# Four buffers for the routing steps' entries and slots, and the last tiles' routing step moved into the tile loop

## The chip, the cores and the metric

The kernel runs on one core of a Trainium2 chip. The metric is device microseconds (us) of one execution, the median of several. The engines are PE (matmul; its weight loads are shown as PEld), DVE (vector), ACT (scalar), POOL (GpSimd) and SP (here it only issues DMAs). Each works through its own queue in order.

## What is computed

One layer of a decoder over 2048 tokens of 1024 features: four token mixers, an output projection with a norm, then a mixture of experts with a gated embedding beside it, and a second norm. The change touches the routing of the experts, which in the reference is

```python
group_p, group_idx = lax.top_k(group_prob, 1)              # best of 4 groups
e_logits = (xt @ w_re + b_re).reshape(t_tok, 4, 8)
e_logits = take_along_axis(e_logits, group_idx[:, :, None], axis=1)[:, 0]
expert_p, local_idx = lax.top_k(softmax(e_logits), 2)      # best two of its 8 experts
gate = group_p * expert_p / sum(expert_p)
expert_idx = group_idx * 8 + local_idx
# ... tokens sorted by expert; each expert's rows: (silu(x Wg) * (x Wu)) Wd, times gate, added up by token
x = LN(alpha * x + HMoE(x) + sigmoid(x W_g + b_g) * (p[i] @ W_p))
```

## The kernel before

The tokens are 16 tiles of 128. After the mixers, `out_proj` (line 1384) makes the first norm's output of all tiles, `ple` (line 1557) makes router logits, gates and embeddings tile by tile and writes each token into the lists of its two experts, and `moe` (line 1851) goes through 32 experts in turns of some 30 us: gate and up weights and down weights are loaded and split into two parts, rows are gathered by the list, multiplied, and added to the rows of `accd` in memory. `finish` is the second norm.

In `ple`, `LATE` is 4, so E = 12 and L = 9. Tiles 0 to 8 go through the loop `for t in range(L)`: `turn` transposes a tile on PE and splits it (ACT, DVE line 52), `gates` multiplies it by the 1060 columns of router and gate in three groups (24 matmuls a group and tile, line 1588; group 0 holds the 36 logits, which line 1592 puts into `r_lg`), `embed` multiplies `p` by its weights and writes the tile to `accd` (lines 1595 to 1611). Tiles 12 to 15 give only their logits, in the turns 1, 3, 5 and 7 of the loop. Tiles 9, 10 and 11 come after the loop: first group 0 of each, then groups 1 and 2 with the embedding of each.

Routing goes by four tiles. `route` (line 1470) is some 40 small DVE instructions and two on ACT: it picks group and experts and fills `r_ent` (token number and gate of 4 tiles x 2 experts) and a one-hot matrix `r_oh`. `route_place` (line 1515) is two matmuls with `r_oh`, some 17 DVE instructions that count slots up to `r_idx`, and 8 indirect DMAs of POOL (line 1541), which scatter the entries `r_ent` to the slots `r_idx` of the lists `listd`. The order of the placings is tiles 0-3, 4-7, 12-15, 8-11. When all are written, `lists` (line 1692) reads the lists' heads back by one DMA of SP (line 1698) into a buffer of the pool `wide`, transposes them on PE (line 1707) and makes the index tables; line 1776 gathers the first expert's rows into another `wide` buffer. That pool has three buffers, which the gates of tiles 9, 10 and 11 hold until their writes to `accd` have landed.

The routing's tiles come from the pool `pw` (line 1562), with one buffer each. So a `route` that writes `r_ent` waits until the 8 scatters of the placing before it have read it.

The order on each engine is not the program's: a planner sets it before the run, by place in the program and by the times of a model, and may take an instruction early where its inputs are ready. Between runtime branches of the experts' stage it moves nothing across.

Of the kernel before, what the change touches and what calls it, by code (L numbers as in the profile page):

```python
# [30 lines left out]
class Layer:  # L31
# [44 lines left out]
    # feature-major column tiles of w_in (start column, width)  # L76
# [4 lines left out]
    # columns that the token shift mixes, with their place in its weights  # L81
# [20 lines left out]
    def proj(self, h, blocks):  # L102
        """one half of the tokens against some of the columns, a block at a time"""
# [91 lines left out]
    # the columns that a causal convolution and silu follow  # L195
    CONV = "mq0", "mq1", "mk0", "mk1"

    def conv(self, i, p, y, more):
        """the taps carry a factor 1/2"""
        nc = self.nc  # L200
        nc.scalar.activation(y, p, AF.Identity, scale=self.cw[:, i, 3:4], bias=self.cb[:, i:i + 1])
        for t in range(3):
            s, w = 3 - t, self.cw[:, i, t:t + 1]
            nc.vector.scalar_tensor_tensor(y[:, s:512], p[:, 0:512 - s], w, y[:, s:512], op0=OP.mult, op1=OP.add)
            if more:
                nc.vector.scalar_tensor_tensor(y[:, 0:s], self.last[:, i, t:3], w, y[:, 0:s], op0=OP.mult, op1=OP.add)
        nc.vector.tensor_copy(self.last[:, i], p[:, 509:512])
        nc.scalar.activation(p, y, AF.Tanh)
        nc.vector.scalar_tensor_tensor(y, p, 1.0, y, op0=OP.add, op1=OP.mult)  # L209

# [62 lines left out]
    def sigmoid(self, out, in_, bias=0.0):  # L273
        """out = 0.5 + 0.5 tanh((in + bias2)/2), bias = bias2 / 2"""
        self.nc.scalar.activation(out, in_, AF.Tanh, bias=bias, scale=0.5)
        self.nc.gpsimd.tensor_scalar(out, out, 0.5, 0.5, op0=OP.mult, op1=OP.add)
# [34 lines left out]
    def rwkv_consts(self):  # L311
# [28 lines left out]
        # masks over [j, i]: same chunk of 64, strict / inclusive, block off the 32-diagonal  # L340
# [19 lines left out]
        # row mu of partition quarter s holds row m = 4 mu + s of the transposed inverse  # L360
# [7 lines left out]
        # products of a tile's tokens, zero between its two chunks  # L368
# [11 lines left out]
    def rwkv_pre(self, q):  # L380
        """scaled operands of the chunks and the inverses of the diagonal 32-blocks"""
# [112 lines left out]
    def rwkv_a(self, q, tt):  # L494
        """token-major operands and the masked products of a tile's chunks, four heads together"""
# [30 lines left out]
    def rwkv_b(self, q, tt):  # L526
        """solves, the chain over the chunks, the tile's outputs"""
# [92 lines left out]
    def rwkv(self):  # L620
        """the group in steps: operands run ahead of the products, and these ahead of the chain"""
# [45 lines left out]
    def log_sigmoid(self, z, out, t):  # L667
        """out = min(z, 0) - ln(1 + exp(-|z|)) for z in SBUF"""
# [22 lines left out]
    def gla_pre(self, q):  # L691
        """queries and keys times their chunk's decays, which go out to memory"""
# [86 lines left out]
    def gla_general(self):  # L779
        """Token by token, for decays too strong for the chunks' common scale."""  # L780
# [67 lines left out]
    def mlstm_gates(self):  # L848
        """gates of all chunks of 128, rows 16 h + c, and the running maxima"""
        nc = self.nc  # L850
        with ExitStack() as ctx:
# [39 lines left out]
            # own chunk's decay on the channels of each head  # L891
# [117 lines left out]
    def rope_tables(self):  # L1009
        """cos and sin (negated for the first half of a head's pairs) of position * frequency, for four heads' rows"""  # L1010
# [36 lines left out]
    def mla_consts(self):  # L1047
# [4 lines left out]
        # the heads' first 64 columns; their rotary columns; these with the pairs swapped  # L1052
# [10 lines left out]
        # the heads' key columns, then their value columns  # L1063
# [16 lines left out]
        # adds the two halves of the rows  # L1080
# [13 lines left out]
    def mla_norms(self, q):  # L1094
        """one over the latents' norms"""
# [22 lines left out]
    def mla_latents(self, q, cn, rs):  # L1118
        """latents over their norms; from them the values of all heads, and their queries and keys, which go out to memory"""
# [62 lines left out]
    def mla_query(self, hd, q):  # L1182
        """queries in two parts with the negated row maxima below them, in steps"""
# [11 lines left out]
        # any value near a row's maximum serves its softmax alike: the leading parts give it  # L1195
# [29 lines left out]
    def mla_attend(self, hd, q):  # L1225
        """even key tiles' products in the upper half of the rows, odd ones' in the lower half, at the same time"""
# [48 lines left out]
    def mla(self):  # L1275
        """the attention of a block of queries in steps, the next block's queries and keys made beside it"""
# [24 lines left out]
        for i, (hd, q) in enumerate(blocks):  # L1301
            while at <= i:
                at = next(ahead, 99)
            for _ in self.mla_attend(hd, q):
                work += self.LEAD
                # a head's keys lie over those of the head before the last
# [12 lines left out]
    ALPHA = 2.0 ** 0.25  # L1319

    def late_pools(self, ctx):
        """first norm's outputs in pairs of tiles, over them later an expert's gate and up weights; transposed blocks"""
# [9 lines left out]
    def weights(self, parts, n, scale=None, pool=None):  # L1332
        """128 rows of weights, put side by side, in leading and trailing parts"""
# [8 lines left out]
    def transpose_split(self, src, hi, lo, spread=False):  # L1342
        """[128, n] to [128, n/128, 128] in leading and trailing parts, rows 0 .. 63 and 64 .. 127 by turns in case of spread"""
# [113 lines left out]
    def pick(self, vals, mx, io, n, k, name):  # L1457
        """lowest index among the entries equal to the maximum, and its one-hot"""
# [11 lines left out]
    def route(self, t0, n, lg):  # L1470
        """tokens of tiles t0 .. t0 + n from logits [128, n, 36]"""
# [28 lines left out]
        ent = w.tile([128, 2, n, 2], F32, name="r_ent")  # L1500
# [14 lines left out]
    def route_place(self, r):  # L1515
        """slots in the experts' lists, behind those of the earlier tiles"""
# [20 lines left out]
        ix = w.tile([128, 2, n], I32, name="r_idx")  # L1537
# [9 lines left out]
    # columns of router and gate side by side, in groups that fill a bank  # L1547
# [9 lines left out]
    def ple(self):  # L1557
        nc, I = self.nc, self.I
        with ExitStack() as ctx:
# [13 lines left out]
            def turn(t):  # L1573
                X[t] = self.turned(self.x1[t]) if t < L + 2 else self.turned(self.x1[t], c)
# [38 lines left out]
            def expert(k, i):  # L1613
                """half of a piece of the first expert's gate and up weights, over rows that are done with"""
# [7 lines left out]
            def logits(t):  # L1622
                """of a tile whose gate comes last; its rows of the experts' sums start from the residual"""
# [14 lines left out]
            for t in range(L):  # L1638
# [11 lines left out]
                if t % 4 == 3:  # L1650
                    r = self.route(t - 3, 4, LG.pop(t // 4))
                if t in (4, 5):
                    expert(0, t % 4)
# [5 lines left out]
            r = self.route(E, 4, LG.pop(E // 4))  # L1659
            gates(L, (0,))  # L1660
            turn(L + 2)
            gates(L + 1, (0,))
            gates(L + 2, (0,))
            self.route_place(r)
# [15 lines left out]
    # of the second norm's tiles: which have their sums taken by ScalarE, and which are scaled by VectorE alone  # L1680
# [4 lines left out]
    NB = 3  # L1685

    def slots(self, ids, gates, idx, gate):
        """a list's entries: token numbers, halved gates"""
# [3 lines left out]
    def lists(self, lt):  # L1692
        """rows of the lists' first blocks: token numbers and gates, one slot per partition"""
# [7 lines left out]
        for j, (i, k) in enumerate(((0, 0), (0, 1), (1, 1), (2, 0))):  # L1701
            if i and k:
                # rows of a full block after one spreading of its columns and after two
# [14 lines left out]
        def pick(j, i):  # L1718
            """part j of the entries for a first block or one of up to 64 rows, part i for others"""
# [11 lines left out]
        # counts in the experts' order of turns, and the higher one of each expert's and the last one's before it  # L1731
# [14 lines left out]
    # experts take turns by group, since the tokens crowd into some of the groups  # L1746
    ORDER = [i % 4 * 8 + i // 4 for i in range(32)]

    def raw_gu(self, e, k):
        """two 128-row pieces of the gate and up weights of the expert that comes in turn e, side by side"""  # L1750
# [28 lines left out]
    def moe_banks(self):  # L1779
        """banks that keep a value when a block is passed over"""  # L1780
# [6 lines left out]
    def passes(self, x, wh, wl, k, half):  # L1787
        """products of the parts; of 64 rows, both parts stand side by side and their products 64 rows apart"""
# [5 lines left out]
    def moe_gu(self, x, W, banks, piece=None, half=False):  # L1794
        """x times gate and up weights, all pieces or one"""
# [8 lines left out]
    def fold(self, p, m):  # L1804
        """adds the lower half's products to the upper half's where m is 1"""
# [6 lines left out]
    def moe_h(self, banks, gate, t=None):  # L1812
        """silu(g) * u * gate, the factor 1/2 of the silu in the gate"""
# [31 lines left out]
    def moe_put(self, y, idx):  # L1845
        """adds rows to those of their tokens; an empty slot's token is out of bounds"""
# [4 lines left out]
    def moe(self, G0=(), x0=None, experts=32):  # L1851
# [8 lines left out]
        def load_counts(t, e, engines):  # L1860
            """four experts' counts, loaded behind the last expert's instructions"""
# [46 lines left out]
        def sized(e, b, f):  # L1908
            """f(False) for more than 64 rows in a block, f(True) for up to 64"""
# [16 lines left out]
        def third(e):  # L1926
            """the third blocks: an expert's products with its down weights and the next one's with gate and up weights"""
# [74 lines left out]
    def moe_general(self):  # L2002
        """the lists' further blocks, for experts with more tokens than the static blocks hold"""
# [48 lines left out]
    def late_x(self, t):  # L2052
        """the first norm's outputs of two tiles whose gates come last"""
# [229 lines left out]
```

## Time and profile before

| | us |
|---|---|
| median of three runs | 3141.1 |
| lowest and highest | 3138.97, 3142.75 |
| span of the profiled execution | 3146.7 |
| PE busy in it, share of the span | 2840.9, 90% |
| logits and gates of tiles 0 to 8, up to | about 1970 |
| tiles 9 to 11 and the lists, from there up to the first expert's first matmul | 2050.87 |

The profiled execution has its span as its only time; it is 5.6 us (0.2%) above the median. In the profile a row of the timeline gives start, length, engine, line of the kernel, operation, what is written and read, and in brackets the engine's idle time just before and what ended it.

### The profile page before, as it was taken

How to read it: one execution, taken by the hardware profiler on the slowest of the kernel's cores; microseconds unless marked ns; L12 is line 12 of the kernel's file. 1: busy time of each engine (PE TensorE's matmuls, PEld its weight loads, DVE VectorE, ACT ScalarE, POOL GpSimd, SP SyncE). 2: the span in 40 equal slices, each digit the busy share in tenths (PEclk: the TensorE clock that was granted, in tenths of full speed). 3: DMA queues.
4: the chain of work that ended last, by engine and by line, in shares of the span. 5: the costliest groups of instructions: out<-in, count | busy, mean ns of one | idle time of the engine just before them, and what ended most of it. 6: DMA issues, size and time to landing. Idle time of an engine off the chain costs nothing. (4 is left out here: it accounts for less than half of the span.)

```text
span 3146.7 us, 42893 instructions
## 1 busy us (share of the span) xinstructions
PE 2840.9 (90%) x15420; PEld 2248.3 (71%) x15421; DVE 1955.0 (62%) x4094; ACT 1225.4 (39%) x2001; POOL 896.7 (28%) x552
## 2 busy tenths in 40 slices
PE   8999999998999899999999998789889988998883
PEld 6888888777877665566577797677667766776662
DVE  6366543566555466766656643467576767666869
ACT  4223232222134332323310121166575756666753
POOL 1000100111010033324421200346355545554525
PEclk9999999999998898989999998899999999999996
DMA  6332143122133612200243412188587867777873
GB/s 189 104 87 75 48 129 92 51 56 59 49 93 132 189 33 69 58 27 17 88 143 132 141 60 60 41 295 275 181 269 233 294 216 237 267 251 225 287 243 134
DMA packets 287054, 443.17 MB, mean 141 GB/s; under 512 B 84088, under 2 KB 152040, under 8 KB 286760
## 3 DMA queue, kind: packets, MB, share of 16 engines
q1 hardware_dynamic: 272200, 397.78, 38.3%
q0 software_dynamic: 14560, 41.47, 5.4%
q8 instruction: 184, 3.01, 0.4%
q14 instruction: 110, 0.90, 0.1%
HBM read 350.52 MB, written 96.50 MB: 142 GB/s over the span
## 5 line engine op out<-in xcount | busy, mean ns | idle before, releaser
L1801 PE MATMUL m_g<-m_g,xhl 128*128 128x512 f32 x2032 | 516.6, 402 | 14.7 <-PEq L1928 8.0
L1801 PEld LDWEIGHTS m_g<-m_g,xhl 128*128 128x128 f32 x2032 | 373.6, 191 | 105.9 <-issue 29.8
L1772 DVE TENSOR_TENSOR m_g<-m_raw,m_g 128x1024 fp32r<-128x1024 f32 x188 | 263.7, 1429 | 124.3 <-ACT m_g L1771 78.9
L1771 ACT CAST m_g<-m_raw 128x1024 fp32r<-128x1024 f32 x252 | 255.3, 1057 | 120.8 <-PEq L1928 105.3
L1833 PE MATMUL m_y<-m_dh,m_h 128*128 128x512 f32 x672 | 236.0, 415 | 24.6 <-PEq L1928 6.1
L59 PE MATMUL pbank<-xh,wh 128*128 128x512 f32 x544 | 220.7, 406 | 11.5 <-DVE us L209 8.2
L60 PE MATMUL pbank<-xl,wh 128*128 128x512 f32 x544 | 219.3, 403 | 0.0
L61 PE MATMUL pbank<-xh,wl 128*128 128x512 f32 x544 | 218.3, 402 | 0.0
L51 ACT CAST xhl<-bank 128x512 fp32r<-128x512 f32 x204 | 118.2, 607 | 251.6 <-PE bank L1350 244.0
L1772 POOL TENSOR_TENSOR m_g<-m_raw,m_g 128x1024 fp32r<-128x1024 f32 x64 | 182.8, 2940 | 89.6 <-ACT m_g L1771 50.5
L1408 PE MATMUL wide<-wt,xhl 128*128 128x512 f32 x768 | 183.4, 397 | 3.6 <-ACT xhl L51 3.6
L1772 POOL TENSOR_TENSOR m_dl<-m_raw,m_dh 128x1024 fp32r<-128x1024 f32 x64 | 177.9, 2814 | 22.1 <-ACT m_dh L1771 21.9
L1833 PEld LDWEIGHTS m_y<-m_dh,m_h 128*128 128x128 f32 x672 | 134.9, 201 | 58.7 <-issue 9.0
L1408 PEld LDWEIGHTS wide<-wt,xhl 128*128 128x128 f32 x768 | 143.7, 189 | 40.1 <-ACT xhl L51 7.4
L1248 POOL TENSOR_TENSOR mla_acc<-mla_acc,mla_pt 128x512 f32<-128x512 f32 (+3 forms) x112 | 135.7, 1212 | 117.4 <-ACT mla_pt L1246 101.1
L52 DVE TENSOR_TENSOR xhl<-bank,xhl 128x512 fp32r<-128x512 f32 x204 | 136.4, 685 | 49.3 <-ACT xhl L51 47.0
L1847 POOL DMA_INDIRECT accd<-m_y,m_put x47 | 94.6, 2013 | 249.6 <-ACT m_y L1840 135.5
L1588 PE MATMUL gate<-wt,xhl 128*128 128x354 f32 (+1 forms) x864 | 152.1, 333 | 14.3 <-DVE wide L1593 7.8
L1246 ACT ACTIVATE mla_pt<-sbank 128x512 f32<-128x512 f32 (+3 forms) x160 | 85.1, 533 | 202.7 <-PE sbank L1242 118.0
L1588 PEld LDWEIGHTS gate<-wt,xhl 128*128 128x128 f32 x864 | 144.1, 193 | 16.5 <-DVE wide L1593 8.6
L1833 PE MATMUL m_y<-m_dl,m_h 128*128 128x512 f32 x376 | 153.9, 409 | 0.0
L59 PE MATMUL pbank<-wh,xh 128*128 128x256 f32 x512 | 151.2, 295 | 0.0
(635 smaller groups left out, 6340.8 us busy)
## 6 DMA issues: line engine op xcount, KB each, us to landing
m_raw<-in_moe_w_down SPq DMA_DIRECT2D x64, 1024.0 KB
m_raw<-in_moe_w_gate SPq DMA_DIRECT2D x126, 512.0 KB
m_raw<-in_moe_w_up SPq DMA_DIRECT2D x126, 512.0 KB
wraw<-in_w_in SPq DMA_DIRECT2D x80, 256.0 KB
o_x<-in_x SPq DMA_DIRECT2D x16, 512.0 KB
x1d<-m_g SPq DMA_DIRECT2D x16, 512.0 KB
accd<-wide SPq DMA_DIRECT2D x16, 512.0 KB
m_raw<-accd SPq DMA_DIRECT2D x7, 1024.0 KB
```

The costliest lines, as they stand in the source:

```text
L51: nc.scalar.copy(hi, src)
L52: (eng and nc.gpsimd or nc.vector).tensor_sub(lo, src, hi.bitcast(F32))
L59: nc.tensor.matmul(out, lh, rh, start=start, stop=False)
L60: nc.tensor.matmul(out, lh, rl, start=False, stop=False)
L61: nc.tensor.matmul(out, ll, rh, start=False, stop=stop)
L1248: (nc.vector if kt in self.SUMS else nc.gpsimd).tensor_add(acc[:, c0 * 128:512], acc[:, c0 * 128:512], pt[:, 0:n])
L1408: nc.tensor.matmul(p[:, j], a[:, k], W[k][bb][:, j * 512:j * 512 + 512], start=k == 0 and i == 0, stop=k == 7 and i == 2)
L1588: nc.tensor.matmul(p[:, 0:n], a[:, k], b[:, o:o + n], start=k == 0 and i == 0, stop=k == 7 and i == 2)
L1771: self.nc.scalar.copy(h[:, i], raw[:, i])
L1772: lo_eng.tensor_sub(l[:, i], raw[:, i], h[:, i].bitcast(F32))
L1801: self.mark["pe"] = self.nc.tensor.matmul(banks[:, j], a, b[:, k % 2, j * 512:j * 512 + 512], start=k == 0 and i == 0, stop=k == 7 and i = ...
L1833: self.nc.tensor.matmul(p[:, j], a, b[:, k % 2, j * 512:j * 512 + 512], start=k == 0 and i == 0, stop=k == 3 and i == len(ps) - 1)
```

## The change

`r_ent` and `r_idx` get four buffers each. The routing of tiles 12 to 15 moves from behind the loop to the end of turn 8 in it, ahead of the first expert's second piece of weights, and its placing moves from behind the logits of tile 11 to ahead of those of tile 10. The calls of `gates`, `embed`, `lists` and the other two routings stay. (The diff also drops comments.)

```diff
-        ent = w.tile([128, 2, n, 2], F32, name="r_ent")
+        ent = w.tile([128, 2, n, 2], F32, name="r_ent", bufs=4)
...
-        ix = w.tile([128, 2, n], I32, name="r_idx")
+        ix = w.tile([128, 2, n], I32, name="r_idx", bufs=4)
...
                 if t % 4 == 3:
                     r = self.route(t - 3, 4, LG.pop(t // 4))
+                if t == L - 1:
+                    r = self.route(E, 4, LG.pop(E // 4))
                 if t in (4, 5):
                     expert(0, t % 4)
                 if t == L - 1:
...
             turn(L)
             turn(L + 1)
-            r = self.route(E, 4, LG.pop(E // 4))
             gates(L, (0,))
             turn(L + 2)
+            self.route_place(r)
             gates(L + 1, (0,))
             gates(L + 2, (0,))
-            self.route_place(r)
             r = self.route(E - 4, 4, LG.pop(E // 4 - 1))
```

## Rows read from the trace of the kernel before

**Rows 1.** The page's first line: the profiled span.

```profile
span 3146.7 us, 42893 instructions
```

**Rows 2.** Waits, 1965 to 2052: waiter <- awaited: total us, times, longest.

```profile
DVE r_ent L1502 <- DMA listd<-r_ent,r_idx: 20.2, 2, 11.2
...
PE gate L1588 <- DVE wide L1593: 7.8, 1, 7.8
...
PE gate L1588 <- DVE xhl L52: 5.8, 1, 5.8
```

**Rows 3.** Windows: stretch, length, busy PE, PEld, DVE, ACT, POOL, clock, DMA.

```profile
1985.00:1990.00 5.00, 0.00 (x0) 0.00 (x0) 0.51 (x5) 0.00 (x0) 0.11 (x1) 0.66 0.01 0
1996.00:2003.00 7.00, 7.00 (x46) 7.00 (x45) 6.80 (x47) 0.42 (x2) 1.92 (x2) 1.00 0.00 0
2015.40:2023.20 7.80, 0.00 (x0) 0.00 (x0) 5.77 (x25) 0.07 (x1) 0.90 (x1) 0.62 0.06 22
```

**Rows 4.** Timeline of DVE: one-hots and entries of 12-15 and 8-11, the lists' first copy.

```profile
1978.17 0.28 DVE L1512 TENSOR_TENSOR r_oh<-r_ohe 128x128 bf16<-128x128 f32 x1
...
1989.49 0.18 DVE L1502 RECIPROCAL r_ent<-r_z 128x4 f32<-128x4 f32 x1 [9.01 <-DMA listd<-r_ent,r_idx]
...
1995.71 0.20 DVE L1592 TENSOR_TENSOR r_lg<-gate,pbias 128x36 f32<-128x36 f32 x1 [4.14 <-PE gate L1588]
...
2002.88 0.29 DVE L1512 TENSOR_TENSOR r_oh<-r_ohe 128x128 bf16<-128x128 f32 x1
...
2017.30 0.18 DVE L1502 RECIPROCAL r_ent<-r_z 128x4 f32<-128x4 f32 x1 [11.24 <-DMA listd<-r_ent,r_idx]
...
2021.86 0.17 DVE L1538 CAST r_idx<-r_sl 128x8 int32<-128x8 f32 x1
...
2037.26 0.29 DVE L1705 COPY wide<-wide 96x256 f32<-96x256 f32 x1 [7.52 <-DMA wide<-listd]
2037.47 1.22 DVE L1610 SCALAR_TENSOR_TENSOR wide<-m_g,wide 128x1024 f32<-128x1024 f32 x1
```

**Rows 5.** Timeline of PE, from the logits of tile 10 to the experts.

```profile
1980.52 4.17 PE L1588 MATMUL gate<-wt,xhl 128*128 128x354 f32 x24
1990.52 5.14 PE L1588 MATMUL gate<-wt,xhl 128*128 128x354 f32 x22 [5.84 <-DVE xhl L52]
...
1995.61 8.02 PE L1588 MATMUL gate<-wt,xhl 128*128 128x354 f32 x48
...
2023.22 0.66 PE L1588 MATMUL gate<-wt,xhl 128*128 128x352 f32 x1 [7.83 <-DVE wide L1593]
...
2037.21 0.76 PE L1707 MATMUL bank<-ident,wide 96*128 96x96 f32 x3 [1.54 <-DMA wide<-listd]
...
2050.87 8.42 PE L1801 MATMUL m_g<-m_g,xhl 128*128 128x512 f32 x36 [0.55 <-DVE m_g L1785]
```

**Rows 6.** Timeline of POOL: scatters of 4-7, 12-15, 8-11, then the gather.

```profile
1973.41 2.82 POOL L1541 DMA_INDIRECT listd<-r_ent,r_idx  x1 [77.46 <-DVE r_idx L1538]
...
1984.15 0.96 POOL L1541 DMA_INDIRECT listd<-r_ent,r_idx  x1 [0.30 <-issue]
...
2009.57 0.96 POOL L1541 DMA_INDIRECT listd<-r_ent,r_idx  x1 [0.30 <-issue]
2022.31 0.96 POOL L1541 DMA_INDIRECT listd<-r_ent,r_idx  x1 [11.77 <-DVE m_tf L1734]
...
2031.16 0.96 POOL L1541 DMA_INDIRECT listd<-r_ent,r_idx  x1 [0.30 <-issue]
2042.60 0.98 POOL L1776 DMA_INDIRECT wide<-x1d,m_idx  x1 [10.48 <-DVE m_mu L1722]
```

**Rows 7.** Timeline of SP's queue: the lists' read, tile 10's write.

```profile
2034.70 0.69 SPq L1698 DMA_DIRECT2D wide<-listd  x1
2038.71 0.35 SPq L1611 DMA_DIRECT2D accd<-wide  x1
```

**Rows 8.** Waits of SP's queue in the experts' stage, 2060 to 2950.

```profile
SPq L1762 <- DVE m_g L1772: 264.0, 29, 27.1
```

## The prediction

> **What bounds the kernel now.** The profiled span is 3146.7 us [rows 1], 5.6 us over the median of the runs; I make the sum against the span and take the same microseconds off the median. PE is busy for 90% of the span, so I looked for the stretches where it is not. The view of the waits between 1965 and 2052 shows three entries that belong together: DVE waits 20.2 us in two goes, ahead of `r_ent`, for scatters to the lists, and PE waits 5.8 and 7.8 us for DVE [rows 2]. The windows show the same as stretches: from 1985 to 1990 PE does nothing, from 2015.4 to 2023.2 again nothing, and the granted clock falls to 0.66 and 0.62, on the way from 2.4 GHz to the lower level [rows 3].
>
> The timeline of DVE says why. At 1989.49 the entries of tiles 12-15 are written after 9.01 us of waiting, because the one buffer of `r_ent` is still read by the scatters of tiles 4-7. At 2017.30 the entries of 8-11 are written after 11.24 us, for the scatters of 12-15 [rows 4]. DVE's queue is in order: behind the first wait stand the splits of tile 11, for which PE waits 5.84 us, and behind the second the rest of the placing of 8-11, the end of tile 9's embedding and the emptying of the gate banks, for which PE waits 7.83 us [rows 5]. After that the chain goes: `r_idx` of 8-11 at 2022.03 [rows 4], eight scatters from 2022.31 to 2032.12 [rows 6], the read of the lists at 2034.70 [rows 7], the lists' transposes at 2037.21 [rows 5], the gather of the first expert's rows at 2042.60 [rows 6], the first expert's product at 2050.87 [rows 5].
>
> In the experts' stage the loads' queue waits for buffers that DVE frees (264.0 us in 29 goes for the down weights alone [rows 8]). The loads do not run late by themselves, so an earlier start of this stage should arrive at the end of the kernel undiminished.
>
> **The change part by part.** *Four buffers for the entries and slots.* No instruction is added. Each of the four routings has its own buffer, so both DVE waits go, and what stands behind them moves up.
>
> First wait: PE ends tile 10's logits at 1980.52 + 4.17 = 1984.69 and could go straight on with the 22 matmuls of tile 11. They took 5.14 us after the idle time; at the 4.17 us for 24 of the row before, 22 take 3.82 [rows 5]. So tile 11's logits end near 1988.5, and the 48 matmuls that began at 1995.61 begin 7.1 us earlier.
>
> Second wait: PE's 7.83 us go too, if DVE then has nothing else in front. DVE's work between the two instants is 5.77 us in 7.80 [rows 3]; without the wait it is done while PE does the gates, long before PE needs the banks. I allow nothing for the clock here. PE's gates, which ended at 2037.21 - 1.54 = 2035.67 [rows 5], then end 7.1 + 7.8 = 14.9 us earlier, at 2020.8.
>
> What is late next? Either PE or the lists. The lists' chain: the logits of tile 11 reach `r_lg` at 1995.91 - 7.1 = 1988.8; from there to the one-hot's end took 7.26 us (1995.91 to 2003.17 [rows 4]), with the placing of 12-15 mixed in, so at most the same: 1996.1. The placing's matmuls stand behind the 48 gate matmuls, so at 1988.5 + 8.0 = 1996.5. From the same point before (1995.61 + 8.02 = 2003.63) to `r_idx` (2022.03) it took 18.4 us, 11.24 of them the wait, so 7.2 remain: 2003.7. The first scatter 0.28 later, the eight take 9.81 (2022.31 to 2032.12), so 2013.8; the read is issued 2.58 after (2032.12 to 2034.70), 2016.4, and its data is used 2.51 after that (to 2037.21), 2018.9 [rows 4 to 7]. PE comes at 2020.8, so PE bounds and the lists have 1.9 us to spare. The transposes move from 2037.21 to 2020.8, by 16.4 us.
>
> From there to the gather it took 5.39 us. The gather writes over tile 10's buffer, whose write to memory was issued at 2038.71, 3.89 us ahead of the gather [rows 6, 7]; that write was late because the end of tile 10's embedding stood on DVE behind the lists' first copy and its 7.52 us of waiting [rows 4]. If the planner keeps that order, the copy comes at 2018.9, the embedding's end at 2020.4, the gather at 2024.3: 18.3 us earlier. If the embedding is no longer behind it, the transposes bound: the gather comes at about half of the 5.39, say 2.7 us, after 2020.8, which is 19.1 us earlier (an estimate; nothing shows that part alone). The clock, which no longer falls in the idle time, gives a little more. I take 19.
>
> *The routing of 12-15 moved into turn 8.* The same instructions, and the planner had them early already: the one-hot of 12-15 was done at 1978.46, ahead of tile 10's logits [rows 4]. Cost 0; bounds: it now stands ahead of the weight splits of turn 8 and of tiles 9 and 10 on DVE, so a PE wait of the size of the 5.84 above could come back at worst, and as much could go.
>
> *The placing of 12-15 moved ahead of tile 10's logits.* Two matmuls on PE of a quarter microsecond together, some 17 DVE instructions which with the routing of 8-11 fill 6.80 of 7.00 us [rows 3], and eight scatters on POOL. The DVE work falls into the time of the first wait, which is then free. On POOL the scatters of 4-7 end at 1985.11 and 12-15 follow directly, to about 1996; those of 8-11 come at 2004, so POOL's queue is free by 8 us. SP's queue is passed by no DMA of this step. Without the move, the scatters of 12-15 would start near 1993 and end near 2003, just in time: the move is cover, the buffers are the gain.
>
> One rule speaks against scatters beside busy vector work. The row: the first scatter of 4-7 took 2.82 us, others 0.96, and three 0.96 ones started while DVE was 6.80 of 7.00 us busy with small instructions [rows 3, 6]. The Trainium skill (SBUF — State Buffer, SBUF: two separate sides) says that GpSimd cannot write the descriptors of its DMAs while DVE holds the shared port in a two-port mode. Here the trace mostly disagrees for the instructions concerned; the rival below prices it.
>
> Sum: 3146.7 - 19 = 3127.7 for the span, 3141.1 - 19 = **3122** for the median. Bounds on the fast side: the 5 us or so that the last steps up to the experts were stretched by waits and the low clock might shrink as well, 27 us in all, 3114.
>
> **The rivals.** *The lists' chain becomes the bound.* For: DVE was let go only 4.38 us after the last scatter of 4-7 was issued (1985.11 to 1989.49) and 6.77 after that of 12-15 (2010.53 to 2017.30) [rows 4, 6]. If SP's read had to wait 6.77 rather than 2.58, the lists land at 2023.1, the embedding's end behind their copy and the gather move with it, and the gain is 14: 3127. Against: SP's own wait is measured at 2.58.
>
> *The scatters slow down beside DVE's work.* At 2.82 instead of 0.96 each, eight cost 14.9 us more, the lists land at 2033.8, the gain is 3.4: 3138; if the eight of 12-15 slow down too, those of 8-11 start late and nothing is left: about 3144. Both are within 0.2%. Against: the row of three above.
>
> *It does not do what it says.* Another single buffer of the routing could hold DVE in its place. The others (`r_ohe`, `r_ee`, `r_oh`) are read by DVE and PE alone, not by scatters, so I give this little: 3141.
>
> *Slower: the experts' stage is ordered anew.* The planner orders every engine by modelled times, and the stage's first instructions now meet other modelled times. There are 31 further turns after the first; from (19 + 6.3) / 31 = 0.8 us a turn the gain is gone and 0.2% more lost. At 1 us a turn: 3141 - 19 + 31 = 3153. Against: the turns' instructions and data are the same, and runtime branches keep the order of each turn apart.
>
> **How the numbers follow.** A measurement of this kernel can tell about 0.2%, 6.3 us, from no change. Forecast 0.60 (3122, its own range 3117 to 3126); more than that, 0.04 (3114 to 3117); lists' chain 0.20 (3126 to 3131); slow scatters 0.05; no effect 0.05; slower 0.06. So faster 0.84, same 0.10, slower 0.06. The range 3114 to 3132 holds the first three.
>
> **What would show it.** No DVE wait for scatters ahead of `r_ent`; PE without its waits of 5.8 and 7.8 us and the clock near 1 from 1985 to the gates' end; the scatters of 12-15 right behind those of 4-7; the lists' read about 2016, the gather about 2023, the first expert's product about 2032, and the experts' stage as long as before. Wrong would be: a new PE wait near 1976 to 1990, a lists' read later than 2020, scatters of over 2 us, or an experts' stage that lengthens.

## The result, and the profile after

The change takes the median from 3140.5 to 3111.1 us (four runs each; the 3141.1 of the forecast was the median of three), runs from 3106.7 to 3116.0 against 3139.0 to 3142.8; the ratio is 0.9899 with a 95% interval of 0.9874 to 0.9923. It was forecast at 3122 with a range from 3114 to 3132: the direction was right, the gain of 29.5 us lies outside the range and is 1.55 times the 19 us forecast.

The profiled execution spans 3112.4 us, the answer to [rows 1]:

```profile
span 3112.4 us, 42881 instructions
```

The timeline of DVE after, which answers [rows 4]: the one-hot of 12-15, tile 11's logits, entries and one-hot of 8-11, their slots, and the lists' first copy with what stands behind it.

```profile
1957.59 0.28 DVE L1512 TENSOR_TENSOR r_oh<-r_ohe 128x128 bf16<-128x128 f32 x1
...
1970.16 0.20 DVE L1592 TENSOR_TENSOR r_lg<-gate,pbias 128x36 f32<-128x36 f32 x1 [2.17 <-PE gate L1588]
...
1975.11 0.18 DVE L1502 RECIPROCAL r_ent<-r_z 128x4 f32<-128x4 f32 x1
...
1975.72 0.29 DVE L1512 TENSOR_TENSOR r_oh<-r_ohe 128x128 bf16<-128x128 f32 x1
...
1984.69 0.17 DVE L1538 CAST r_idx<-r_sl 128x8 int32<-128x8 f32 x1
...
1999.75 0.30 DVE L1706 COPY wide<-wide 96x256 f32<-96x256 f32 x1 [5.57 <-DMA wide<-listd]
1999.95 1.22 DVE L1610 SCALAR_TENSOR_TENSOR wide<-m_g,wide 128x1024 f32<-128x1024 f32 x1
```

Ahead of `r_ent` at 1975.11 no wait stands in brackets any more, and none stands ahead of the other writes of `r_ent` either. PE after, which answers [rows 5]: the placing's matmuls of 12-15 (line 1523) now stand inside tile 10's logits, 87 gate matmuls follow without a gap, and the transposes of the lists (here line 1708, since the changed kernel has one line more) follow the gates at once.

```profile
1962.19 1.38 PE L1588 MATMUL gate<-wt,xhl 128*128 128x354 f32 x7
1963.41 0.23 PE L1523 MATMUL bank<-r_oh,lower 128*128 128x128 bf16 x1
...
1963.50 14.39 PE L1588 MATMUL gate<-wt,xhl 128*128 128x354 f32 x87
...
1992.69 7.43 PE L1588 MATMUL gate<-wt,xhl 128*128 128x352 f32 x45
1999.95 0.50 PE L1708 MATMUL bank<-ident,wide 96*128 96x96 f32 x3
...
2014.08 9.32 PE L1802 MATMUL m_g<-m_g,xhl 128*128 128x512 f32 x36
```

POOL's scatters and the gather, which answer [rows 6], and SP's two DMAs, which answer [rows 7]:

```profile
1954.53 1.70 POOL L1541 DMA_INDIRECT listd<-r_ent,r_idx  x1 [61.61 <-DVE r_idx L1538]
1956.54 1.36 POOL L1541 DMA_INDIRECT listd<-r_ent,r_idx  x1 [0.30 <-issue]
...
1968.27 0.96 POOL L1541 DMA_INDIRECT listd<-r_ent,r_idx  x1 [2.81 <-DVE r_idx L1538]
...
1985.14 0.96 POOL L1541 DMA_INDIRECT listd<-r_ent,r_idx  x1 [7.03 <-DVE m_tf L1735]
...
1993.98 0.96 POOL L1541 DMA_INDIRECT listd<-r_ent,r_idx  x1 [0.30 <-issue]
2005.09 0.98 POOL L1777 DMA_INDIRECT wide<-x1d,m_idx  x1 [10.15 <-DVE m_mu L1724]
```

```profile
1997.24 0.68 SPq L1699 DMA_DIRECT2D wide<-listd  x1
2001.20 0.35 SPq L1611 DMA_DIRECT2D accd<-wide  x1
```

All of this happened as forecast (the 3.5 us for which PE waits for a split at 1957.72 stood in the same place before, 3.0 us at 1976.06), but everything in it is already some 19 us early at its beginning. So the rest of the gain lies ahead of 1965, in the loop. The waits of DVE from 1780 to 2060 in the kernel before have one more row beside that of [rows 2], of the same tile but another line:

```profile
DVE r_ent L1507 <- DMA listd<-r_ent,r_idx: 17.1, 1, 17.1
```

Line 1507 copies token numbers, which are constants, into `r_ent`. The planner put the copy for tiles 4-7 early into DVE's queue, right behind a split of turn 5, when the scatters of tiles 0-3 had just begun to read the one buffer. The timeline of DVE before, that of PE before, then the same place of PE after:

```profile
1888.07 1.29 DVE L52 TENSOR_TENSOR xhl<-bank,xhl 128x512 fp32r<-128x512 f32 x2 [0.84 <-ACT xhl L51]
1906.47 0.24 DVE L1507 COPY r_ent<-tok 128x4 f32<-128x4 f32 x2 [17.10 <-DMA listd<-r_ent,r_idx]
```

```profile
1907.35 5.28 PE L1631 MATMUL gate<-wt,xhl 128*128 128x36 f32 x24 [12.12 <-DVE wide L1593]
1912.46 2.05 PE L1607 MATMUL pv<-wt,p_ph 128*128 128x512 f32 x4
...
1916.87 1.05 PE L1607 MATMUL pv<-wt,p_pl 128*128 128x512 f32 x2
```

```profile
1892.11 2.82 PE L1631 MATMUL gate<-wt,xhl 128*128 128x36 f32 x24
1894.78 1.19 PE L1607 MATMUL pv<-wt,p_ph 128*128 128x512 f32 x4
...
1897.19 0.63 PE L1607 MATMUL pv<-wt,p_pl 128*128 128x512 f32 x2
```

Behind the copy stood the emptying of the gate banks, for which PE waited 12.12 us. Then it ran slowly: the 24 matmuls took 5.28 us and after the change 2.82, the 12 behind them 5.46 (1912.46 to 1917.92) and 3.04 (1894.78 to 1897.82). The wait was 12.1 us of idle time and was followed by 4.9 us of slow work, 17.0 together. The windows (stretch, length, busy time of PE, PEld, DVE, ACT, POOL, granted clock, DMA) show the clock in the same place, before and after:

```profile
1907.35:1919.60 12.25, 12.25 (x48) 10.98 (x49) 4.01 (x7) 3.17 (x4) 0.00 (x0) 0.55 0.00 1
```

```profile
1891.50:1899.20 7.70, 7.70 (x55) 7.01 (x53) 4.34 (x9) 3.45 (x5) 1.12 (x2) 1.00 0.23 38
```

A clock of 0.55 is nearly the lower level of 1.2 GHz, 1.00 the upper of 2.4 GHz. Not all of the slow work needs the wait: the next group of such matmuls, 24 of line 1631 and 12 of line 1607, took 5.70 us at a clock of 1.00 before (from 1947.84) and 7.27 at 0.77 after (from 1927.46), behind 0.23 us of idle time in both. So some 1.6 of the 17.0 us come back there.

### The profile page after: what moved, and what is told of

It is laid out like the page before. It is cut to its first block, busy times and chain, and to the rows that moved or that the text cites. A ratio compares the mean times of both kernels' runs of the same rounds, so it can differ in the third digit from the quotient of the medians.

```text
span 3112.4 us, 42881 instructions
## 1 busy us (share of the span) xinstructions
PE 2830.1 (91%) x15420; PEld 2239.0 (72%) x15421; DVE 1949.2 (63%) x4094; ACT 1224.5 (39%) x2001; POOL 892.6 (29%) x552
## 5 line engine op out<-in xcount | busy, mean ns | idle before, releaser
L1246 ACT ACTIVATE mla_pt<-sbank 128x512 f32<-128x512 f32 (+3 forms) x160 | 85.0, 532 | 200.6 <-PE sbank L1242 116.8
L60 PE MATMUL pbank<-wl,xh 128*128 128x256 f32 x512 | 150.0, 293 | 0.0
```

Source lines behind the costliest of these rows:

```text
L60: nc.tensor.matmul(out, lh, rl, start=False, stop=False)
```

## The experiments

The kernel can be cut by events that all versions have: the placing's first matmul of tiles 0-3 (line 1523; 1877.6 before), that of tiles 4-7 (1965.1) and the first expert's first product (2050.87). The early wait lies in the stretch A between the first two, the two forecast waits in B between the second and third, the experts and the second norm in C behind. From the traces, in us, in the order of the text:

| kernel | up to A | A | B | C | median | ratio to before (95%) |
|---|---|---|---|---|---|---|
| before | 1877.6 | 87.5 | 85.8 | 1095.9 | 3140.5 | |
| before, second trace | 1886.5 | 87.2 | 83.8 | 1095.3 | one run, 3154.8 | |
| changed | 1874.5 | 71.7 | 67.8 | 1098.3 | 3111.1 | 0.9899 (0.9874 to 0.9923) |
| changed, second | 1867.9 | 71.7 | 68.0 | 1093.2 | 3112.4 | 0.9908 (0.9888 to 0.9929) |
| changed, third | 1875.0 | 74.8 | 69.7 | 1094.6 | one run, 3116.2 | |
| own buffer for 4-7 | 1872.2 | 76.5 | 83.4 | 1094.5 | 3133.8 | 0.9973 (0.9957 to 0.9989) |
| only 4-7 without | 1878.7 | 87.2 | 71.3 | 1095.2 | 3130.5 | 0.9954 (0.9934 to 0.9975) |
| buffers alone | 1876.3 | 76.5 | 71.0 | 1095.8 | 3116.5 | 0.9924 (0.9895 to 0.9953) |
| buffers alone, second | 1889.2 | 74.8 | 71.3 | 1095.1 | one run, 3132.2 | |
| move alone | 1881.1 | 85.9 | 84.5 | 1091.5 | 3142.0 | 1.0005 (0.9988 to 1.0023) |
| token numbers late | 1876.6 | 73.3 | 86.5 | 1090.1 | 3128.9 | 0.9957 (0.9938 to 0.9975) |
| two buffers | 1870.7 | 71.7 | 76.2 | 1090.5 | 3117.1 | 0.9935 (0.9916 to 0.9953) |
| four of entries, one of slots | 1868.7 | 71.7 | 68.2 | 1094.8 | 3110.3 | 0.9903 (0.9881 to 0.9925) |
| rows gathered elsewhere | 1877.3 | 74.8 | 70.6 | 1091.6 | 3119.9 | 0.9928 (0.9902 to 0.9954) |

The means of the two traces before and the three after differ by 87.35 - 72.73 = 14.6 us in A and 84.8 - 68.5 = 16.3 in B, 30.9 together; the medians differ by 29.5. So the two stretches hold the whole gain, about half each, and C passes it on.

**The early wait alone.** The theory is that the gain not forecast is this wait; the rival, that it comes from elsewhere. In one kernel only tiles 4-7, 12-15 and 8-11 share a second buffer, so that the early wait goes and the late ones stay; the other is the complement. (`own` is the same ending, handed from `route` to `route_place`.)

```diff
-        ent = w.tile([128, 2, n, 2], F32, name="r_ent")
+        ent = w.tile([128, 2, n, 2], F32, name="r_ent" + {0: "", 4: "b", 12: "b", 8: "b"}[t0])
...
-        ix = w.tile([128, 2, n], I32, name="r_idx")
+        ix = w.tile([128, 2, n], I32, name="r_idx" + own)
```

> The kernel before, with a second buffer of entries and slots that tiles 4-7, 12-15 and 8-11 share. So the entries of 4-7 no longer wait for the scatters of 0-3, and the two later waits stay. Theory (the part of the gain that was not forecast is a third wait, 17.1 us of DVE at 1889 to 1906 of the kernel before, in which PE stood 12.1 us and came back at the lower clock): the DVE wait there is gone, the other two keep their 9 and 11 us, and the time falls by 15 to 17 us, to about 3124. Rival (the unforecast part comes from elsewhere, as from the order on the engines in the experts' stage, or from scatter between runs): under 5 us less, 3136 or more.

Measured: the ratio gives 4 to 13 us, with the middle at 8.5; the trace gives 10.9 in A (87.35 to 76.5) and the late waits still there with 17.6 us. The rival's 5 us at most lie at the very end of the interval; the 15 to 17 us are missed as well. Where a part of them stayed is seen at the place itself:

```profile
1891.39 4.01 PE L1631 MATMUL gate<-wt,xhl 128*128 128x36 f32 x24 [1.52 <-DVE r_lg L1592]
```

PE was held for 1.52 us, though DVE waited for no DMA there, and ran slowly again behind it. The same short wait, 1.39 to 1.50 us, stands in both traces of the buffers alone, in the third of the changed kernel and in the last kernel of the table (A 74.8 to 76.5), and not in the others that are rid of the early wait (A 71.7 in four traces, of three programs, and 73.3 in one). A has 74.8 in one trace of the changed kernel and 71.7 in two, so a part of this is not the program's.

The complement, with the endings `{0: "", 4: "", 12: "b", 8: "c"}`:

> The complement: entries of 0-3 and 4-7 share one buffer, 12-15 and 8-11 have one each, and nothing is moved. Theory: the wait of 17.1 us at 1889 stays, the two later ones go; the time falls by what was forecast for these, 14 to 19 us, to about 3123. If the move of the placing carries a part of it, less: 10 us, 3131. Rival (the late waits are not what bounds the stage): under 5 us.

Measured: 14.5 us by the ratio (8 to 21), 13.5 in B. The early wait stayed in full, and PE's wait with it:

```profile
DVE r_ent L1507 <- DMA listd<-r_ent,r_idx: 16.2, 1, 16.2
...
PE gate L1631 <- DVE wide L1593: 11.5, 2, 11.2
```

So the late waits alone are worth 13.5 to 14.5 of the 19 us that were forecast, and nothing of that needs the move.

**Why the early wait exists.** One buffer each, nothing moved; only the copy of the token numbers is made to depend on the routing it belongs to:

```diff
-            nc.vector.tensor_copy(ent[:, k, :, 0], self.tok[:, t0:t0 + n])
+            nc.vector.scalar_tensor_tensor(ent[:, k, :, 0], ix, 0.0, self.tok[:, t0:t0 + n], op0=OP.mult, op1=OP.add)
```

> One buffer each, nothing moved; the copy of the token numbers into the entries is replaced by an operation that also reads the chosen expert's number (times zero), so that it can't stand in DVE's queue ahead of the routing it belongs to. Theory (the early wait exists only because the copy of a constant was put early into the queue; the buffer itself is free by the time the routing of 4-7 needs it): no wait near 1889, the two later ones as before, about 3124 as with a buffer of its own. Rival (the routing needs the second buffer anyway): the wait moves to the routing and the time stays at 3140.

Measured: 13.5 us less by the ratio (8 to 20), a median of 3128.9 where about 3124 was expected, A at 73.3 and B not shorter than before, at 86.5. The early wait is gone without any buffer, the late ones stand (waits, then PE at the place):

```profile
DVE r_ent L1502 <- DMA listd<-r_ent,r_idx: 21.5, 2, 11.4
```

```profile
1894.14 2.82 PE L1631 MATMUL gate<-wt,xhl 128*128 128x36 f32 x24
```

The order of the instructions on PE, ACT, POOL and SP is that of the kernel before; on DVE only these copies stand elsewhere. So this is shown: the early wait came from a copy of constants that the planner had put ahead of its use, and the routing of 4-7 itself never needed the second buffer.

**Buffers and move apart.** The buffers without the move, then the move without the buffers:

> Four buffers, nothing moved. Theory (the buffers are the gain, the move is cover): within 4 us of the changed kernel, 3111 to 3115; the scatters of 12-15 then start behind tile 11's logits, some 7 us later than with the move, and end just as those of 8-11 are due. Rival (the move carries the late part): 3118 to 3125, with the late scatters queued behind those of 12-15 and the lists' read later than PE's gates.

> The move alone, one buffer each. Theory (the waits stay): the 17.1 us wait at 1889 as before, about 9 us ahead of the entries of 12-15, and a shorter one ahead of those of 8-11, since the scatters of 12-15 start earlier: 3131 to 3141, faster by 0 to 9 us. Rival (the move is a half of the gain): 3126 or less.

Measured: the buffers alone reach a ratio of 0.9924, whose interval overlaps that of the whole change; the median, 3116.5, is 1.5 us above what was expected. By the ratios the early and the late waits by themselves add up to 23 us, the buffers alone give 24 and the whole change 29 to 32. The move alone does nothing that can be measured. Its waits:

```profile
DVE r_ent L1507 <- DMA listd<-r_ent,r_idx: 23.9, 2, 15.9
...
DVE r_ent L1502 <- DMA listd<-r_ent,r_idx: 6.4, 1, 6.4
```

They add up to 30.3 us against 37.3 before. A second look at three of the kernels:

> Four buffers without the move, for a second trace: 41.5 and 116.3 us in the first. Theory (the move is worth 1 to 3 us in the second stretch; the 3 to 5 us more in the first were a stall that no engine of this program causes): 37 to 42 and 115 to 117. Rival (the move carries nothing): 113 to 115 in the second.

> The kernel before, once more, for a second trace. From the logits' 10390th matmul to the 10620th (around the wait near 1889) it took 53.9 us, from there to the first expert's product 131.3, the experts and the second norm 1095.8. Theory (the two stretches are set by the waits, the rest scatters): within 2 us in the first two; the part of the kernel ahead of them, 1865.6, and that behind them differ by up to 7 us from run to run with the same program. Rival (the part ahead of them is shortened by the change by some 6 us, since it was 1856 to 1863 in all four traces with the move and the buffers, and 1862 to 1871 in the other five): 1864 to 1868 again.

> The changed kernel, for a third trace. Theory: the two stretches 36 to 38 and 113 to 116 us as in its other traces, the part ahead of them anywhere from 1855 to 1871. Rival: that part at 1856 to 1863 again.

These three expectations cut the kernel a little differently: at PE's 10390th and 10620th matmul, around the early wait, and at the first product. By that cut the second trace before has 52.0 and 131.0, as forecast; the third of the changed kernel 39.6 and 116.8, which is 1.6 and 0.8 us above what was expected; the second of the buffers alone 39.6 and 118.4, the latter 1.4 us above. By the cut of the table B is 71.0 and 71.3 with the buffers alone and 67.8, 68.0 and 69.7 with the move, so the move is worth some 2.6 us on top of the buffers, by the traces only. Most of this can be seen: without the move PE, done with the gates, waits 1.23 and 3.05 us for the lists' read, in the three traces of the changed kernel not at all, and the gates end 54.7 us behind the placing of 4-7 without the move and 54.8 with it, in the means.

The part up to the 10390th matmul, whose instructions stand in the same order in all versions (copies of token numbers apart), was meant to be told apart by these runs and was not: 1874.6 before and 1877.2 with the buffers alone are above all that either side gave, 1863.1 in the changed kernel is within both. Over all 14 traces it is 1860 in the mean of the six with the move and more than one buffer of entries (1856 to 1865) and 1868 in the mean of the other eight (1860 to 1877), where four traces that lack 11 earlier matmul records are cut 11 matmuls earlier. A chance of the profiled runs or not, the medians have no room for 7 us more than A and B give.

**How many buffers, and of what.** Two of each in place of four, then four of the entries and one of the slots:

> The change with two buffers each in place of four. Theory: each routing then waits for the scatters of the last but one, which have ended some 7 us or more before in the changed kernel's trace; same time as with four, 3107 to 3116. Rival (the release comes up to 6.8 us after the last scatter, as before the change, so two are too few): 2 to 6 us more, with a DVE wait ahead of the entries of 8-11.

> The change with four buffers of entries and one of slots. Theory: the slots are written late in the placing, so that only those of 12-15 and 8-11 meet scatters still running (4-7's last is issued at 1965.5, 12-15's slots are written at 1967.8), a wait of up to 5 us each on DVE that PE does not see or sees little: 0 to 6 us more than the changed kernel, 3111 to 3117. Rival (the slots' buffers do half of the work): 3124 or more.

Measured: two buffers lose, by the trace. A is as good (71.7), B is 76.2, 7.7 us over the changed kernel's mean; the ratio's middle is 0.9935 against 0.9899 and 0.9908, but the intervals overlap, so that the times alone would not tell. The same copy does it again, now for 8-11, whose turn it is on the buffer of 4-7. DVE and PE:

```profile
1965.88 0.24 DVE L1507 COPY r_ent<-tok 128x4 f32<-128x4 f32 x2 [7.54 <-DMA listd<-r_ent,r_idx]
```

```profile
1966.76 0.26 PE L1523 MATMUL bank<-r_oh,lower 128*128 128x128 bf16 x1 [7.06 <-DVE xhl L52]
```

The expectation of the same time was wrong for the reason of the forecast: it asked when the routing needs the buffer, and not where its earliest write stands in the queue. With one buffer of slots nothing is lost: the two waits are 3.9 us together, one of them

```profile
1964.13 0.17 DVE L1538 CAST r_idx<-r_sl 128x8 int32<-128x8 f32 x1 [2.27 <-DMA listd<-r_ent,r_idx]
```

and B is 68.2. So the entries' buffers are the change.

**Spread, and a try for more.** The changed kernel once more:

> The changed kernel once more, for its spread and for a like comparison with the runs beside it. Theory: 3107 to 3116, 29 to 30 us under the kernel before. Rival (the first runs were lucky): 3118 or more.

The median was 3112.4 and the runs went from 3102.6 to 3122.4, wider than the first four. In the last kernel the first expert's rows are gathered into another free buffer, since the gather had seemed to wait for tile 10's write:

```diff
-            x0 = self.wide.tile([128, 1060], F32, name="wide")[:, 0:1024]
+            x0 = self.g_tile()[:, 0].bitcast(F32)
```

> The changed kernel, with the first expert's rows gathered into a buffer of the gate and up weights that is free by then, in place of the buffer of tile 10's gate. Theory (the gather, 3.1 us behind the list's index table, waits for tile 10's write to memory): it starts some 2.5 us earlier, PE's wait of 4.0 us for it shrinks to 1.5, and the experts start 2 to 3 us earlier: 3108 to 3110 against 3111. Rival (the gather waits for the index table or for POOL alone): no earlier, the same time.

POOL and PE of it:

```profile
2012.38 0.98 POOL L1777 DMA_INDIRECT m_g<-x1d,m_idx  x1 [8.23 <-ACT p_ph L51]
```

```profile
2018.18 1.94 PE L1350 MATMUL bank<-ident,m_g 128*128 128x128 f32 x8 [3.57 <-DMA m_g<-x1d,m_idx]
```

The gather starts 3.45 us behind the lists' transposes (2008.93) where it was 5.14 (1999.95 to 2005.09), 1.7 earlier; but its rows are used 5.80 us later (2012.38 to 2018.18) where it was 4.43 (2005.09 to 2009.52). From the transposes to the first product it is 13.8 us against 14.1: the buffer was part of the wait, and freeing it brings nothing worth having. The median of 3119.9, where 3108 to 3110 was expected, is not better either.

## Why the prediction was wrong, step by step

*What bounds the kernel now* is the step that failed. It took the waits between 1965 and 2052, found two ahead of `r_ent`, 20.2 us [rows 2], and the sum then said that "both DVE waits go". A view of all waits of the tile would have shown three; the third is 17.1 us long and lies at 1889. The stretch was chosen by where the routing of 12-15 and 8-11 stands, while the sentence "each of the four routings has its own buffer" already said that the change reaches the routing of 4-7. The term that was missing is 14.6 us, by the two traces before and the three after; 11.3 of it is idle time of PE and 3.1 slow work in the two groups of 36 matmuls.

*The two late waits* were right in mechanism and somewhat large in size: 19 us forecast, 16.3 measured over the traces, 18.0 in the first pair, some 2.6 of it by the move. Measured from the placing of 4-7 (1965.1 before, 1946.3 after) the steps came out as forecast: the lists' read at 51.3 us forecast and 51.0 measured, the gather at 58.4 to 59.2 and 58.8, the first product at about 67 and 67.8. That the gather came out so near is partly luck. The gates ended 53.9 us behind the placing where 55.7 was forecast, and from the transposes to the gather it took 5.14 us where 2.7 to 3.5 was: two errors of about 2 us that cancel. PE was the bound, as said, but only just: the gates ended at 2000.1, the lists' copy at 1999.75 had waited 5.57 us for its data. The spare time of the lists was 0.4 us and not the 1.9 forecast (0.7 and 0.1 in the other two traces). The end of tile 10's embedding did stay behind that copy.

*Cost of the move:* forecast at nothing, called cover. Alone it measures nothing, with the buffers 2.6 us by the traces. That is right in kind: without it PE waits for the lists, so it is cover that was needed.

*The rivals.* The lists' chain did not become the bound, since SP issued the read 2.30 us after the last scatter (1994.94 to 1997.24), near the 2.58 of before; without the move it did, by the 1.23 and 3.05 us above. The scatters did not slow down, but for the first two of 4-7: these took 1.70 and 1.36 us, the others 0.95 to 0.99, with DVE 8.26 of 12.00 us busy beside those of 12-15:

```profile
1965.00:1977.00 12.00, 12.00 (x76) 12.00 (x75) 8.26 (x48) 0.42 (x2) 7.20 (x8) 1.00 0.02 1
```

What made those longer can be read from the traces. DVE before the change, at the first scatter of 4-7 (1973.41 to 1976.23 [rows 6]):

```profile
1973.02 1.24 DVE L1610 SCALAR_TENSOR_TENSOR wide<-m_g,wide 128x1024 f32<-128x1024 f32 x1
1974.16 1.24 DVE L52 TENSOR_TENSOR m_g<-wide,m_g 128x1024 fp32r<-128x1024 f32 x1
```

The scatter began inside the first of these and ended 0.83 us behind the second. Of the 448 scatters of the 14 traces, 35 took 1.36 us or more, and these are the ones that began while DVE ran an operation of these two kinds, over 128x1024 elements with both inputs in SBUF, the memory on the chip. The operation of line 1609 is as large, but one of its inputs is `pv`, which PE writes and which lies in PSUM: 23 scatters ran beside it, at 0.96 us each. The Trainium skill (SBUF — State Buffer, SBUF: two separate sides) says that a DVE operation with two SBUF inputs, once it has started, keeps the port that it shares with GpSimd from a GpSimd operation that reads SBUF. The trace agrees, by these 35 and 23, for the scatters, which read entries and slots there; in this stage it cost no time. The prediction had taken the trace to disagree mostly with the skill: the rule that it named is that of the two-port mode, of which no run here shows whether an operation was in it, and in its window of 7.00 us two scatters began (2000.72 and 2001.98) and not three.

The experts' stage was not ordered to its loss: C is 1095.4 in the mean of the three and 1095.6 before.

*The range* left no room for a wait in another place. It was built from bounds on the rows that had been read, and the error was in which rows had been read. Its fast end is also not the sum that it is said to be: 19 and 5 us make 24 and not 27, so 3117 and not 3114. The measured 3111 lies outside both.

*What stays open:* why the part up to A takes from 1868 to 1889 us in traces of the same instructions, and whether the change has a hand in it. That A itself came at 71.7, 73.3, 74.8 and 76.5 without a long wait can be told from the traces, though not its cause. It has two groups of 24 matmuls of line 1631 and 12 of line 1607. A group takes 5.7 us at a clock of 1.00, and 7.2 to 8.9 where the clock fell for a part of it, as to 0.77 in the 7.27 us above. At 71.7 one of the two was slow, at 73.3 both were, and at 74.8 and 76.5 the wait of 1.39 to 1.52 us ahead of the first comes on top. In that wait ACT and SP start late as well as DVE; what held all three is not shown. The medians need neither, since A and B together give 30.9 us where the medians differ by 29.5.

## What to carry to other kernels

When a tile gets more buffers, list every wait of every write to it over the whole run before adding up: the change acts on all of them, and not only where the idle time was noticed. A copy of constants into a shared buffer is dangerous under a planner, since it is ready first, is put early into an in-order queue, and holds up everything behind it until the buffer is free; making it depend on the data it goes with took 13.5 us off here by itself, and a second buffer for it 8.5. An idle stretch of the matmul engine can be worth more than its length: 12.1 us of waiting were followed by 4.9 us more in slow matmuls, of which some 1.6 came back at a later place when the wait was gone.

## What the runs showed of the hardware that was not expected

A scatter of 128 small entries is issued in 1.27 us on POOL, but the time from the last issue of eight to the release of the engine that waits for them differs widely: in the kernel before, DVE was let go 10.5 us after the scatters of 0-3 (1895.96 to 1906.47), 4.4 after those of 4-7 and 6.8 after those of 12-15, while SP waited 2.6 and, after the change, 2.3 us. Over all traces that have such waits it differs by the series far more than within one: 9.3 to 10.5 us for DVE after 0-3, 3.1 to 4.8 after 4-7, 5.2 to 7.0 after 12-15, and 1.8 to 2.7 for SP after 8-11. What makes the difference was not tried. The spread of whole runs was also wider than the first four told: the kernel before ran from 3128 to 3158 us in one of the later comparisons, and the changed one from 3103 to 3122.
